# An up projection by Strassen's scheme: seven half-block products in place of eight, in an encoder layer on one core

## The chip, the cores and the metric

The kernel runs on one core of a Trainium2 chip. The metric is the device time of one execution in microseconds (us); three runs of the kernel before took 3004.14, 3004.00 and 2998.63 us, median 3004.0. The engines go by the names of the profile: PE is TensorE (matrix products; PEld is its loading of the stationary operand), DVE is VectorE, ACT is ScalarE, POOL is GpSimd, SP is the engine that issues most DMAs.

## The reference, cut to what matters

The layer is a mixing part (a state-space branch and an attention branch) and a feed-forward part. Only the feed-forward part is changed in what it computes with:

```python
def conv_ffn_sublayer(x, norm_g, w_up, conv_w, conv_b, w_down):
    n = rms_norm(x, norm_g).astype(w_up.dtype)
    h = n @ w_up                                   # (tokens, 1024) @ (1024, 5632)
    h = depthwise_conv3(h, conv_w) + conv_b        # over tokens, zero beyond either end
    g, up = jnp.split(h, 2, axis=-1)               # 2816 + 2816 columns
    act = silu(g) * up
    return x + act @ w_down                        # (2816, 1024)
```

It is applied to a prompt of 256 tokens and to a sample of 2048 tokens with the same weights (2304 tokens in all). Everything is float32.

## The kernel before, in words

A product of two float32 matrices is made of three TensorE products: each operand is split into a high part (rounded to `F32R`) and a low part (what is left), and hi.hi, lo.hi and hi.lo are summed in PSUM (`mm3`, lines 151 to 154). To split costs one ACT copy (high) and one DVE subtraction (low).

After the attention, a stage of the output projection takes the 18 tiles of 128 tokens one by one (`prepare`, `scale_b`, `project_b`, `second_norm`, lines 1213 to 1290; the order is `TOKS`). `second_norm` normalises a tile, transposes it on TensorE (tile `ptn`) and splits it into the tiles `n2a` (prompt and the first 1152 tokens, kept in SBUF) or, for the rest, by way of DRAM into `n2b`.

The up projection (lines 1293 to 1342, tiles named `pu`) then loops over 22 column tiles `ct`, and in each over 5 blocks of tokens: one of 512 columns and four of 450 (with the neighbours that the convolution reads). For each block and each of the two halves `j` (gate and up), 24 matmuls (8 row blocks of the weights, three products each) sum in one PSUM bank; ACT multiplies by the middle tap and adds the bias on the way out of PSUM (L1329), DVE adds the two outer taps straight from PSUM (L1332, L1335), then ACT makes the silu (L1338), DVE the product (L1339), and a DMA writes the result `act_d`. `up_weight` (lines 1170 to 1179) loads one 1024x128 piece of `w_up` (`us`, 512 KB), multiplies it by the norm's gains on DVE (L1176) and splits it (L1177, L1178). It is called for `ct + 1` ahead of the products of `ct`, so each weight is loaded and split once: 44 pieces.

The down projection (tiles named `pf`, lines 1353 to 1386) follows: 2376 matmuls of 512 columns, with `down_weight` for its weights.

All instructions are ordered by a planner at build time that works through a list in the order of the program and gives an engine its next instruction when the operands are ready in its own estimate of time; the order within each engine is fixed from then on, and waits between engines are put in by it. A buffer of a pool (`bufs=`) is reused once all that used it are done.

## Time and profile before

| what | us |
|---|---|
| median of the runs (lowest, highest) | 3004.0 (2998.63, 3004.14) |
| span of the profiled execution | 2999.1 |
| first matmul of the up projection | at 1325.4 |
| first matmul of the down projection, straight behind the last of the up projection | at 2445.1 |
| PE busy in the span | 2901.1 (97%) |
| DVE, ACT, POOL busy in the span | 1555.8, 1048.5, 509.2 |

The profile gives the span of the one execution it was taken in, and no other time for that execution; the span lies inside the spread of the runs. Busy times of PE overlap one another (a matmul is counted from start to the modelled end of its pipeline), so the rate of matmuls is read from how many start in a stretch, not from their durations.

### The profile page before, as it was taken

What the parts mean: (1) busy time and instruction counts of PE and PEld (TensorE: products, weight loads), DVE (VectorE), ACT (ScalarE), POOL (GpSimd) and SP (SyncE); (2) the same over time, 40 slices, a digit from 0 to 9 for tenths busy, and PEclk for the clock granted to TensorE, in tenths of its full rate; (3) what the DMA queues carried; (4) which work ended last, traced back from release to release, by engine and by line L of the source; (5) the groups of instructions that cost most, each with busy time, mean ns of one, the idle gap of its engine ahead of it and who ended that gap; (6) DMA issues with size and microseconds to landing.
All of it is one profiled execution on the core that took longest, in us unless ns stands there. A gap on an engine that the chain in (4) does not pass through costs nothing.

```text
span 2999.1 us, 41529 instructions
## 1 busy us (share of the span) xinstructions
PE 2901.1 (97%) x15224; PEld 2475.5 (83%) x15224; DVE 1555.8 (52%) x4006; ACT 1048.5 (35%) x2390; POOL 509.2 (17%) x946
## 2 busy tenths in 40 slices
PE   7998999989899999999999999999999999999999
PEld 7887777778788887888898989898888888888887
DVE  5766899976644545774444444444444442223221
ACT  3444455445665664452222222222222230002000
POOL 0588433221343343110000000000000000000000
PEclk9998999998999999999999999999999999999999
DMA  7564878595769775664111111111111142224221
GB/s 217 181 222 129 263 223 245 169 222 121 173 155 186 170 167 171 223 202 146 54 37 50 40 51 40 50 39 48 41 44 46 44 154 88 83 84 133 84 80 49
DMA packets 407064, 369.19 MB, mean 123 GB/s; under 512 B 84801, under 2 KB 352717, under 8 KB 403789
## 3 DMA queue, kind: packets, MB, share of 16 engines
q1 hardware_dynamic: 384012, 316.18, 36.2%
q0 software_dynamic: 22848, 50.35, 7.0%
q8 instruction: 121, 1.98, 0.3%
q14 instruction: 83, 0.67, 0.1%
HBM read 228.93 MB, written 137.53 MB: 122 GB/s over the span
## 4 chain that ended last, share of the span: by engine, by line
PE 70%; DMA 4%; DVE 2%; ACT 2%; issue 0%; POOL 0%; SPq 0%; DVEq 0%; ACTq 0%; POOLq 0%
PE pu L153 12%; PE pu L154 12%; PE pu L152 12%; PE pf L153 6%; PE pf L154 6%; PE pf L152 6%; PE po L996 3%; PE pt L149 2%; PE s L959 2%; PE s L960 2%; PE ppa L152 1%; PE ppa L153 1%; PE ppa L154 1%; DMA wsoa<-in_w_out_dram 1%; DMA wb<-w_d 1%; DMA x<-x_d 1%
## 5 line engine op out<-in xcount | busy, mean ns | idle before, releaser
L1332 DVE SCALAR_TENSOR_TENSOR h<-pu,convp,h 128x448 f32<-128x448 f32 (+3 forms) x264 | 162.4, 616 | 554.8 <-ACT h L1329 554.8
L152 PE MATMUL pu<-n2a,uw 128*128 128x450 f32 (+1 forms) x1056 | 398.1, 377 | 0.9 <-ACT n2a L1237 0.9
L153 PE MATMUL pu<-n2a,uw 128*128 128x450 f32 (+1 forms) x1056 | 398.5, 377 | 0.4 <-DVE n2a L1238 0.4
L154 PE MATMUL pu<-n2a,uw 128*128 128x450 f32 (+1 forms) x1056 | 398.1, 377 | 0.0
L1329 ACT ACTIVATE h<-pu,convp 128x448 f32<-128x448 f32 (+2 forms) x220 | 161.9, 736 | 632.5 <-PE pu L154 632.4
L153 PE MATMUL pf<-dw,ah 128*128 128x512 f32 x792 | 310.9, 393 | 0.0
L154 PE MATMUL pf<-dw,ah 128*128 128x512 f32 x792 | 310.5, 392 | 0.0
L152 PE MATMUL pf<-dw,ah 128*128 128x512 f32 x792 | 310.2, 392 | 0.0
L153 PE MATMUL pu<-n2b,uw 128*128 128x450 f32 x704 | 258.8, 368 | 0.0
L154 PE MATMUL pu<-n2b,uw 128*128 128x450 f32 x704 | 258.7, 367 | 0.0
L152 PE MATMUL pu<-n2b,uw 128*128 128x450 f32 x704 | 258.6, 368 | 0.0
L1381 DVE TENSOR_TENSOR acc<-pf,acc 128x512 f32<-128x512 f32 x72 | 49.7, 691 | 390.6 <-PE pf L154 390.6
L153 PEld LDWEIGHTS pu<-n2a,uw 128*128 128x128 f32 x1056 | 199.6, 189 | 28.6 <-DVE n2a L1238 0.8
L152 PEld LDWEIGHTS pu<-n2a,uw 128*128 128x128 f32 x1056 | 198.6, 188 | 28.9 <-ACT n2a L1237 1.1
L154 PEld LDWEIGHTS pu<-n2a,uw 128*128 128x128 f32 x1056 | 199.2, 189 | 27.0
L1367 ACT ACTIVATE ah<-at 128x512 fp32r<-128x512 f32 x72 | 53.0, 784 | 420.5 <-PE pf L154 420.5
L966 ACT ACTIVATE sb<-sb,st 128x256 f32<-128x256 f32 (+2 forms) x384 | 172.3, 451 | 29.7 <-DVE st L965 28.0
L153 PEld LDWEIGHTS pf<-dw,ah 128*128 128x128 f32 x792 | 148.3, 187 | 35.2 <-DVE dw L1192 0.4
L152 PEld LDWEIGHTS pf<-dw,ah 128*128 128x128 f32 x792 | 148.3, 187 | 35.1
L154 PEld LDWEIGHTS pf<-dw,ah 128*128 128x128 f32 x792 | 148.3, 187 | 34.5
L1335 DVE SCALAR_TENSOR_TENSOR h<-pu,convp,h 128x448 f32<-128x448 f32 (+1 forms) x264 | 162.8, 617 | 7.8
L959 PE MATMUL s<-kh,qs 128*128 128x256 f32 (+2 forms) x384 | 151.5, 402 | 0.0
(603 smaller groups left out, 6116.2 us busy)
## 6 DMA issues: line engine op xcount, KB each, us to landing
at<-act_d SPq DMA_DIRECT2D x36, 704.0 KB
us<-in_w_up_dram SPq DMA_DIRECT2D x44, 512.0 KB
qk_d<-qt SPq DMA_DIRECT2D x72, 256.0 KB
act_d<-h SPq DMA_DIRECT2D x66, 224.0 KB
wb<-w_d SPq DMA_DIRECT2D x32, 384.0 KB
ds<-in_w_down_dram SPq DMA_DIRECT2D x44, 256.0 KB
ph_d<-ph SPq DMA_DIRECT2D x16, 640.0 KB
phl<-ph_d SPq DMA_DIRECT2D x16, 640.0 KB
```

The lines of the kernel that those rows point to most:

```text
L149: T.transpose(out, in_, ident[:n, :n])
L152: mm = T.matmul(ps, lhi, rhi, start=first, stop=False)
L153: T.matmul(ps, lhi, rlo, start=False, stop=False)
L154: T.matmul(ps, llo, rhi, start=False, stop=last)
L959: T.matmul(ps[:, c:c + n], qs[:, q], khi[:, keys], start=True, stop=False)
L960: T.matmul(ps[:, c:c + n], qs[:, q], klo[:, keys], start=False, stop=True)
L966: A.activation(sb[:, c:c + n], sb[:, c:c + n], AF.Exp, bias=mn, scale=-1.0, accum_out=den)
L996: T.matmul(po[half * ST:(half + 1) * ST], v, pb_[:s, half * n + j, :], start=j == 0, stop=j == n - 1)
L1329: A.activation(h[:, a:b], ps[:, a:b], AF.Identity, bias=cw[:, 3], scale=cw[:, 1])
L1332: V.scalar_tensor_tensor(h[:, a1 + o:b1], ps[:, a1 + o - 1:b1 - 1], cw[:, 0], h[:, a1 + o:b1], ALU.mult, ALU.add)
L1335: V.scalar_tensor_tensor(h[:, a1:b1 - o], ps[:, a1 + 1:b1 + 1 - o], cw[:, 2], h[:, a1:b1 - o], ALU.mult, ALU.add)
L1367: A.activation(ahl[:, 0, c0:c1], at[:, c0:c1], AF.Copy)
```

## The change

The tokens are taken in three groups of 768 (`GROUPS`: the prompt with tokens 0 to 511, then 512 to 1279, then 1280 to 2047), and the loop over the 22 column tiles runs inside the loop over the groups. In each of the 66 steps the gate and the up tile of a group (2 x 128 columns of weights, 2 x 512 rows, 2 x 384 tokens) are made of seven products of half blocks in place of eight (Strassen's scheme in Winograd's form): each product is 4 row blocks by three matmuls of 384 columns. The sums of weight blocks are made on GpSimd, the sums of token blocks on VectorE and GpSimd once per group, and the results are put together by sums in PSUM, ACT copies and DVE additions into rows `rg` and `ru` of 768 tokens in SBUF. The convolution reads these rows rather than PSUM; the two last columns of a group are kept in `edges` for the next. The gains of the norm go onto the tokens in `second_norm` instead of onto the weights, and that step no longer splits: it multiplies out of PSUM into `raw` (first group) or writes 256 KB pieces to DRAM (other groups). The weights are loaded, summed and split in each of the three groups anew. `TOKS` is in another order. Comments were removed, and a 64-byte pad was added.

```diff
-NSP = 1152
+GT = 768
+GN = GT // 2
+NG = NT // GT
-    TOKS = [16, 17] + list(range(8, 16)) + list(range(8))
+    TOKS = [16, 17] + list(range(4)) + list(range(8, 12)) + list(range(4, 8)) + list(range(12, 16))
+    GROUPS = [[16, 17, 0, 1, 2, 3], list(range(4, 10)), list(range(10, 16))]
-    wp_u = [ctx.enter_context(mkpool(name="wu0", bufs=2))]
+    wp_u = [ctx.enter_context(mkpool(name="wu0", bufs=4))]
+    wst_v = pu.enter_context(mkpool(name="wstv", bufs=2))
+    wsum = pu.enter_context(mkpool(name="wsum", bufs=1))
+    ORDER = (1, 5, 6, 2, 7, 3, 4)
+    def up_weight(nm, ct):
+        w = []
+        for j in range(2):
+            c0 = j * DFF + ct * P
+            s = (wst_u, wst_v)[j].tile([P, KD, P], F32, name=f"us{nm}{j}", tag="us")
+            nc.sync.dma_start(out=s, in_=w_up[0, :, c0:c0 + P].rearrange("(k p) c -> p k c", p=P))
+            w.append(s)
+        a11, a12, a21, a22 = w[0][:, 0:4], w[0][:, 4:8], w[1][:, 0:4], w[1][:, 4:8]
+        sm_ = wsum.tile([P, 4, 4, P], F32, name=f"su{nm}", tag="su")
+        s1, s2, s3, s4 = (sm_[:, i] for i in range(4))
+        G.tensor_tensor(s1, a21, a22, ALU.add)
+        G.tensor_tensor(s2, s1, a11, ALU.subtract)
+        G.tensor_tensor(s3, a11, a21, ALU.subtract)
+        G.tensor_tensor(s4, a12, s2, ALU.subtract)
+        src = {1: a11, 2: a12, 3: s4, 4: a22, 5: s1, 6: s2, 7: s3}
...
+            out[m] = wp_u[i >= 4].tile([P, 2, 4, P], F32R, name=f"uw{nm}{m}", tag="uw")
+            split_in(out[m], src[m])          # ACT copy (high), DVE subtraction (low), 512 columns
...
+    def right_operands(g):                    # token blocks, split_in of 1536 columns each
+        put(1, b11)
+        V.tensor_tensor(b11, b12, b11, ALU.subtract)
+        put(5, b11)
+        V.tensor_tensor(b11, b22, b11, ALU.subtract)
+        put(6, b11)
+        put(2, b21)
+        G.tensor_tensor(b12, b22, b12, ALU.subtract)
+        put(7, b12)
+        put(3, b22)
+        G.tensor_tensor(b21, b21, b11, ALU.subtract)
+        put(4, b21)
...
+            product(p, 1, wt, True, False)
+            A.activation(rg[:, lo], p, AF.Copy)
+            product(q, 5, wt, True, False)
+            A.activation(ru[:, hi], q, AF.Copy)
+            product(p, 6, wt, False, False)
+            A.activation(rg[:, hi], p, AF.Copy)
+            product(t, 2, wt, True, True)
+            V.tensor_tensor(rg[:, lo], t, rg[:, lo], ALU.add)
+            product(p, 7, wt, False, False)
+            V.tensor_tensor(ru[:, hi], p, ru[:, hi], ALU.add)
+            product(q, 3, wt, False, True)
+            V.tensor_tensor(rg[:, hi], q, rg[:, hi], ALU.add)
+            product(p, 4, wt, False, True)
+            A.activation(ru[:, lo], p, AF.Copy)
...
+                A.activation(h[:, a:b], r[:, a:b], AF.Identity, bias=cw[:, 3], scale=cw[:, 1])
+                    V.scalar_tensor_tensor(h[:, c0:c1], r[:, c0 - 1:c1 - 1], cw[:, 0], h[:, c0:c1],
+                    V.scalar_tensor_tensor(h[:, c0:c1], r[:, c0 + 1:c1 + 1], cw[:, 2], h[:, c0:c1],
```

The tile `p` takes four products in turn in one PSUM bank (1, then 6, 7 and 4 added on top); between them it is copied or added out, so the next product on `p` waits for that. `p` and `q` share a pool of 4 banks, `t` has 3. The rows, `h` and the loads of weights have two buffers each, the four weight sums (`wsum`) one, the seven token operands one.

## Rows read from the trace of the kernel before

**Rows 1.** Busy time by stretch: up projection, then down projection.
```profile
core 0: us, PE busy (x) PEld busy (x) DVE busy (x) ACT busy (x) POOL busy (x), PEclk, DMA share, GB/s
1500.00:2400.00 900.00, 900.00 (x4267) 804.75 (x4266) 391.80 (x581) 215.29 (x302) 0.00 (x0) 1.00 0.14 44
2460.00:2990.00 530.00, 529.99 (x2293) 428.90 (x2292) 123.33 (x151) 62.79 (x81) 0.00 (x0) 1.00 0.29 89
```
**Rows 2.** Who waited for whom, longest in total first (engine line <- releaser).
```profile
ACT h L1329 <- PE pu L154: 632.4, 198, 9.8
DVE h L1332 <- ACT h L1329: 554.8, 213, 5.5
```
**Rows 3.** Order of time, attention: TensorE at 256 columns (start, us, engine).
```profile
696.34 0.30 PE L153 MATMUL pg<-zlo,ghi 128*128 128x256 f32 x1
696.36 0.19 PEld L154 LDWEIGHTS pg<-zhi,glo 128*128 128x128 f32 x1
...
696.48 0.28 PE L154 MATMUL pg<-zhi,glo 128*128 128x256 f32 x1
696.49 0.19 PEld L152 LDWEIGHTS pg<-zhi,ghi 128*128 128x128 f32 x1
...
696.60 0.28 PE L152 MATMUL pg<-zhi,ghi 128*128 128x256 f32 x1
696.60 0.19 PEld L153 LDWEIGHTS pg<-zlo,ghi 128*128 128x128 f32 x1
696.72 0.28 PE L153 MATMUL pg<-zlo,ghi 128*128 128x256 f32 x1
```
**Rows 4.** First matmuls of the up and the down projection (ns min/median/max, starts).
```profile
L152 PE MATMUL pu<-n2a,uw x1056: 360/369/482, 1325.4 to 2424.7; 128*128 128x450 f32 x110, 128*128 128x512 f32 x66
L152 PE MATMUL pf<-dw,ah x792: 388/394/400, 2445.1 to 2994.1; 128*128 128x512 f32 x198
```
**Rows 5.** Order of time, end of attention: DVE operations back to back.
```profile
1194.45 0.68 DVE L1035 TENSOR_TENSOR ot<-ot,ot 128x512 f32<-128x512 f32 x1
1195.05 0.74 DVE L165 SCALAR_TENSOR_TENSOR olob<-wsob,gains,ohib 128x512 fp32r<-128x512 f32 x1
1195.72 0.68 DVE L1035 TENSOR_TENSOR ot<-ot,ot 128x512 f32<-128x512 f32 x1
```
**Rows 6.** Groups by line and shape, DVE (count, busy us, mean ns).
```profile
L1381 DVE TENSOR_TENSOR acc<-pf,acc 128x512 f32<-128x512 f32 x72 | 49.7, 691 | 390.6 <-PE pf L154 390.6
L1178 DVE TENSOR_TENSOR uw<-us,uw 128x1024 fp32r<-128x1024 f32 x44 | 53.4, 1215 | 0.0
L1368 DVE TENSOR_TENSOR ah<-at,ah 128x512 fp32r<-128x512 f32 x36 | 24.9, 691 | 0.0
```
**Rows 7.** The same view, ACT.
```profile
L1367 ACT ACTIVATE ah<-at 128x512 fp32r<-128x512 f32 x36 | 22.7, 631 | 420.5 <-PE pf L154 420.5
L949 ACT ACTIVATE pb<-pt 128x384 f32<-128x384 f32 x30 | 14.5, 483 | 8.9 <-DVE pb L950 8.9
L557 ACT ACTIVATE junk<-xt 128x1024 bf16<-128x1024 f32 x18 | 19.0, 1057 | 30.3 <-DMA xt<-in_x_sample_dram 27.4 <-DMA xt<-in_x_prompt_dram 3.0
```
**Rows 8.** POOL: additions of two SBUF operands (line: count, min/median/max ns; groups).
```profile
L1035 POOL TENSOR_TENSOR ot<-ot,ot x30: 1263/1282/1709, 772.7 to 1187.4; 128x512 f32<-128x512 f32 x30
L1257 POOL TENSOR_TENSOR ot<-ot 128x256 f32<-128x256 f32 x18 | 13.3, 737 | 95.8 <-ACT ot L1256 95.8
```
**Rows 9.** Order of time, POOL and DVE beside each other.
```profile
1221.08 0.46 POOL L1258 TENSOR_TENSOR ot<-ot 128x128 f32<-128x128 f32 x1
...
1221.17 0.38 DVE L142 SCALAR_TENSOR_TENSOR rb8t<-rb8y 128x1 f32<-128x1 f32 x1
1221.48 0.15 DVE L142 SCALAR_TENSOR_TENSOR r216t<-r216y 128x1 f32<-128x1 f32 x1
```
**Rows 10.** Lines L165 (both operands in SBUF) and L873 (one in PSUM): min/median/max ns.
```profile
L165 DVE SCALAR_TENSOR_TENSOR olob<-wsob,gains,ohib x8: 739/896/1895, 1175.8 to 1206.3; 128x512 fp32r<-128x512 f32 x8
...
L873 DVE SCALAR_TENSOR_TENSOR pxt<-ppa,rab,pxt x32: 734/749/752, 823.9 to 1198.4; 128x512 f32<-128x512 f32 x32
```
**Rows 11.** Busy time by stretch, columns as in rows 1: the output projection ahead.
```profile
1210.00:1326.00 116.00, 112.60 (x565) 93.78 (x565) 92.56 (x424) 65.22 (x107) 19.18 (x32) 1.00 0.71 232
```
**Rows 12.** Order of time, DVE: a load of weights, waited for.
```profile
2042.29 1.22 DVE L1176 TENSOR_TENSOR us<-us,gains 128x1024 f32<-128x1024 f32 x1 [0.83 <-DMA us<-in_w_up_dram]
```
**Rows 13.** Order of time, SP: the issue of that load.
```profile
2038.47 7.18 SPq L1173 DMA_DIRECT2D us<-in_w_up_dram  x2
```

More of the change, by code (lines that the diff above doesn't have):

```diff
@@ L112, in tile_encoder @@
     x1_d = scratch("x1_d", [NT, D])
[L113 removed]
+    n2_d = [[[scratch(f"n2_d{g}{k}{h}", [P, 4, GN]) for h in range(2)] for k in range(2)] for g in range(1, NG)]
     act_d = scratch("act_d", [NCT, P, NT])
@@ L1189, in down_weight @@
             nc.sync.dma_start(out=s[:, i], in_=w_down[0, r0:r0 + P, h * 512:(h + 1) * 512])
+        if pool is wp_u[0]:
+            for i in range(2):
+                hl = pool.tile([P, 2, 4, P], F32R, name=f"dw{half}{e}{i}", tag=tag)
+                hl = hl.rearrange("p s k c -> p s (k c)")
+                split_in(hl, s[:, i])
+                downw[divmod(e + i, KF)] = hl
+            return
         hl = pool.tile([P, 2, 2, 512], F32R, name=f"dw{half}{e}", tag=tag)
-        A.activation(hl[:, 0], s, AF.Copy)
-        V.tensor_tensor(hl[:, 1], s, hl[:, 0].bitcast(F32), ALU.subtract)
+        split_in(hl, s)
         for i in range(2):
@@ L1288, in tile_encoder @@
         if i == 4:
-            upw = {(0, j): up_weight(0, j) for j in range(2)}
+            upg = up_weight("0_0", 0)
+            upw = next(upg)
     second_norm(*prev)
@@ L1294, in tile_encoder @@
         return
+    wp_u.append(pu.enter_context(mkpool(name="wu1", bufs=6)))
+    n2bp = pu.enter_context(mkpool(name="n2b", bufs=1))
     hpool = pu.enter_context(mkpool(name="hp", bufs=2))
[L1298 to L1302 removed]
@@ new lines, in tile_encoder, with put @@
+    edges = [hpool.tile([P, 2, NCT, 2], F32, name=f"edge{g}", tag=f"edge{g}", bufs=1) for g in range(NG - 1)]
+    right_ops = {}
+    def right_operands(g):
+        (b11, b12), (b21, b22) = raw
+        def put(m, src):
+            pool = n2pool if m in ORDER[:4] else n2bp
+            right_ops[m] = pool.tile([P, 2, 4, GN], F32R, name=f"no{g}{m}", tag=f"no{m}")
+            split_in(right_ops[m], src)
+        put(1, b11)
[9 more added lines that the diff above has]
+        put(4, b21)
@@ new lines, in product @@
+    def product(ps, m, w, first, last):
+        r = right_ops[m]
+        for k in range(4):
+            for i, (a, b) in enumerate(((0, 0), (0, 1), (1, 0))):
+                T.matmul(ps, w[m][:, a, k], r[:, b, k], start=first and k == 0 and i == 0,
+                         stop=k == 3 and i == 2, skip_group_check=True)
+    next(upg)
+    for g in range(NG):
+        right_operands(g)
+        if g + 1 < NG:
+            for k in range(2):
+                for h in range(2):
+                    raw[k][h] = n2pool.tile([P, 4, GN], F32, name=f"rb{g}{k}{h}", tag=f"rb{k}{h}")
+                    nc.sync.dma_start(out=raw[k][h], in_=n2_d[g][k][h])
+        for ct in range(NCT):
+            wt = upw
+            if (g, ct) != (NG - 1, NCT - 1):
+                for upw in up_weight(*((f"{g}_{ct + 1}", ct + 1) if ct + 1 < NCT else (f"{g + 1}_0", 0))):
+                    pass
+            else:
+                for e in (0, 2):
+                    down_weight(0, e, wp_u[0], "uw")
+            rg, ru = [hpool.tile([P, 2 + GT], F32, name=f"r{g}_{ct}{j}", tag=f"r{j}") for j in range(2)]
+            lo, hi = slice(2, 2 + GN), slice(2 + GN, 2 + GT)
+            p = psm.tile([P, 512], F32, name=f"pu{g}_{ct}p", tag="pw")[:, :GN]
+            q = psm.tile([P, 512], F32, name=f"pu{g}_{ct}q", tag="pw")[:, :GN]
+            t = pst.tile([P, 512], F32, name=f"pu{g}_{ct}t", tag="pt")[:, :GN]
+            product(p, 1, wt, True, False)
[12 more added lines that the diff above has]
+            A.activation(ru[:, lo], p, AF.Copy)
+            hv = []
+            a = 1 if g else 2
+            b = GT + 2 if g == NG - 1 else GT + 1
+            for j, r in enumerate((rg, ru)):
+                if g:
+                    G.tensor_copy(r[:, 0:2], edges[g - 1][:, j, ct])
+                if g + 1 < NG:
+                    G.tensor_copy(edges[g][:, j, ct], r[:, GT:GT + 2])
+                cw = convp[:, :, j * NCT + ct:j * NCT + ct + 1]
+                h = hpool.tile([P, 2 + GT], F32, name=f"h{g}_{ct}{j}", tag=f"h{j}")
+                A.activation(h[:, a:b], r[:, a:b], AF.Identity, bias=cw[:, 3], scale=cw[:, 1])
+                for c0, c1 in ((3, 2 + NP), (3 + NP, b)) if g == 0 else ((a, b),):
+                    V.scalar_tensor_tensor(h[:, c0:c1], r[:, c0 - 1:c1 - 1], cw[:, 0], h[:, c0:c1],
@@ L1333, in tile_encoder @@
                                            ALU.mult, ALU.add)
-                    o = 1 if last else 0
-                    V.scalar_tensor_tensor(h[:, a1:b1 - o], ps[:, a1 + 1:b1 + 1 - o], cw[:, 2], h[:, a1:b1 - o],
+                for c0, c1 in ((2, 1 + NP), (2 + NP, b)) if g == 0 else ((a, min(b, GT + 1)),):
+                    V.scalar_tensor_tensor(h[:, c0:c1], r[:, c0 + 1:c1 + 1], cw[:, 2], h[:, c0:c1],
                                            ALU.mult, ALU.add)
```

86 lines of the change are left out of this document (22 added, 64 removed).

## The prediction

> **What bounds the kernel now.** I read the view of busy time by stretch first. In the up projection TensorE is never idle, DVE is busy 44% of the time, ACT 24%, POOL not at all, and the clock is granted in full [rows 1]. The list of waits says the same from the other side: the longest waits are ACT for the last matmul of a block and DVE for ACT [rows 2]. So only the number and the rate of matmuls count here, and everything else hides under them. The rate: 4267 matmuls start in 900 us, 210.9 ns each at a mean of 462.4 columns (one block of 512, four of 450); in the down projection 2293 in 530 us, 231.1 ns at 512 columns [rows 1]. At 256 columns three starts take 0.38 us, 127 ns each [rows 3]. The line through 256 and 512 columns rises 0.408 ns a column and gives 210.9 at 462.4, so it holds in between: at 384 columns a matmul takes 127 + 128 x 0.408 = **179 ns**.
>
> **PE: removed and added.** Before: 22 x 5 x 2 x 24 = 5280 matmuls, 5280 x 0.2109 = 1113.6 us; the stage lasts from 1325.4 to 2445.1 [rows 4], 1119.7 us, so 6.1 us of it are the last tiles of the output projection, woven in. After: 66 steps x 7 products x 12 = 5544 matmuls, 84 a step, 15.03 us a step, 992 us in all. That is 121.6 us less, the most that the change can bring. The seven-for-eight would bring 139 at equal width; the narrower matmul gives some of it back.
>
> Whether a narrower matmul still hides the loading of its weights is the first doubt. In the up projection PEld is busy 804.75 of 900 us, 189 ns for each of 4266 loads [rows 1]; if they were strictly serial, a step could not be under 84 x 0.189 = 15.9 us. But at 256 columns loads of 0.19 us start every 0.12 us [rows 3], so they overlap, and I take 179 ns. The Trainium skill (Trainium Kernel Development and Optimization, Best Practices) would have the distance to the roofline judged by the busy share of LDWEIGHTS; by that rule the stage is at 89% already and the change would bring little. That is a rival below; the rows at 256 columns speak against it.
>
> **DVE per step.** Durations overlap when queued, so I use starts: an addition of 512 columns takes 0.60 us, a scaled addition (scalar_tensor_tensor) 0.67 us [rows 5]; a further column costs (1215 - 691)/512 = 1.02 ns, and an operand in PSUM costs the same as one in SBUF, 691 ns at 512 columns [rows 6]. So a step has seven splits of 512 columns, 7 x 0.60 = 4.2; three additions out of PSUM of 384 columns, 3 x 0.47 = 1.4; four taps of 768 columns, 4 x 0.93 = 3.7; one product of 768 columns, 0.86. Sum 10.2 us of 15.03. Gone is the multiplication by the gains (1.22 us a piece, [rows 12]); the rest is what grew. ACT: seven copies of 0.63, four of 384 columns at 0.48, two taps and a silu of 768 columns at about 0.63 + 256 x 0.83 ns = 0.85 [rows 7], the tap with up to 0.15 more: 4.4 + 1.9 + 2.7, 9 us, 60%: covered, unless it is held by something else.
>
> **POOL per step, and the port.** Four sums of 512 columns at 1.28 us [rows 8], 5.1 us. POOL had nothing to do here, and this is what I look at hardest. A DVE operation on a 128x1 operand takes 0.15 us, but 0.38 when a POOL addition has just begun, and then ends with it [rows 9]. A split with both operands in SBUF takes 739 ns at best and 1895 at worst, which is one POOL addition more; the like with one operand in PSUM never exceeds 752 though POOL works beside it too [rows 10]. So DVE operations with two SBUF operands and POOL additions exclude each other. In the new step 8.8 of DVE's 10.2 us are of that kind. If POOL always runs while DVE is idle or on its PSUM additions, the port is taken 8.8 + 5.1 = 13.9 us and a step stays at PE's 15.03; if DVE waits out every POOL addition, it needs 10.2 + 5.1 = 15.3. Both ends lie around PE's own time. I take 15.3, since [rows 9, 10] show DVE waiting to the end: 66 x 15.3 = 1010. In the first group the taps are cut in two at the prompt's end, four starts more (0.67 - 0.52 = 0.15 each), 0.6 us in 22 steps; half of it counted, 6. The Trainium skill (GPSIMD Engine Reference, 4.1 Engine selection) sends elementwise work to VectorE, with GpSimd about 2 times slower on two inputs; here 1.28 against 0.69, so the trace agrees. With the sums on DVE (4 x 0.60) a step would need 12.6 us of DVE and no port, and PE would bound.
>
> **Between groups.** The seven token operands are split anew: seven splits and two sums of 1536 columns at 0.60 + 1.05 = 1.65, 14.8 us of DVE, and two POOL sums of 1.28 + 1024 x 2.1 ns = 3.5 us (2.1 ns a column from 256 and 512 columns, [rows 8]). Each operand has one buffer, so its split waits for the last step's product on it; the DVE queue holds the last step's convolution behind it, and PE waits for it in turn. From both sides: nothing (the last step's slack and the two row buffers take it) to 21.8 us. With the port as full as above there is no slack: 14.8 plus half of POOL's 7, **18 us**, twice, 36. The loads of the next group's tokens stand in SP's queue ahead of the weights of the next step, and wait until the operands are made; a load of 512 KB is 3.8 us from issue to use [rows 12, 13], and there are two buffers, so this hides within the same 18. At the start of the first group four operands can be made during the output projection, where DVE has 23 us free in 116 [rows 11]; three must wait for its memory, but have four products (8.6 us) of cover. Between 0 and 18, I take 5. The hand-over to the down projection: weights for it could be loaded under the last blocks, now the memory is freed in the last step. One output block of its first tile (33 x 0.231 = 7.6 us) is the price at most, 0 at least; 3.
>
> **The rest.** The output projection loses two ACT copies per tile and gains DRAM writes; PE is busy 112.6 of 116 us there [rows 11], so between 3 us won and as much lost (DVE has then four splits of operands more); 0. The order of tiles changes which rows are ready first, and nothing waits for them by more than that. Weights are read three times, 1 MB in 15 us; the DMA engines are 14% busy here [rows 1], about three and a half times that afterwards: hidden.
>
> **Sum.** 1010 + 6 + 36 + 5 + 3 + 6 = 1066 us, against 1119.7: 54 us less. On the profiled execution 2999.1 - 54 = 2945; the median of the runs is 4.9 above that span, so 3004.0 - 54 = **2950 us**.
>
> **Rivals.** (a) PE bounds throughout: POOL's sums fall into DVE's gaps, boundaries cost 5 us each: 992 + 10 + 6 + 4 = 1012, 2896 us. For it: the two loads (13.9 and 10.2 us) are below 15.03; against: the gaps would have to fit to within 8%. (b) Slower: orders fixed at build time collide. `p` is freed for product 4 by a DVE addition that has one product, 12 x 0.179 = 2.15 us, to be done in, and the earlier products on `p` by ACT copies in the same time. If at its head DVE has a split behind a POOL sum (1.28 + 0.60), a tap (0.93) and its own 0.47, that is 3.3 us and PE loses 1.1 us in a step; with two POOL sums in the way 2.4. Above 16.2 us a step ((1119.7 - 50)/66) the gain is gone; at 17 it is 1122 + 50 = 1172, 52 slower, **3056 us**. For it: POOL's four sums come in a burst once `wsum` is free, and DVE then gets one operation between two of them. Against: PE's wait gives DVE the time to catch up, so it can't build up. (c) Weight loads serial: 66 x 15.9 = 1049, with 36 + 14 it is 1099, 2983 us. (d) The boundaries and SP's queue eat all: two times 45 us, 3004 us.
>
> **How the numbers follow.** Forecast (2920 to 2990) 0.44, (a) 0.22, (b) 0.23, (c) 0.06, (d) 0.05. A difference within 0.2%, 6 us, can't be told from none here. Faster is forecast, (a) and (c), 0.72; same is (d), 0.05; slower is (b), 0.23. The range takes in (a), and (b) to some 16.9 us a step: 2888 to 3048; the forecast alone is 2920 to 2990.
>
> **What would show it.** The rate: 384-column matmuls start 179 ns apart inside a product; 189 would be (c). The port: POOL's sums longer than 1.28 us or DVE splits of 1.2 to 1.9 us; PE's waits in a step are for ACT copies or DVE additions of the rows, under 0.5 us a step in sum for the forecast, none for (a), over 1.2 for (b). Boundaries: two holes on PE of 10 to 20 us in all, waiting for `no`. I am wrong if the step is far from 15.3, and in the reason if PE waits for something else than DVE's and POOL's work: weights in DMA, or ACT held at the head of its queue.

## The result

The changed kernel takes 2952.5 us (median of four runs, 2951.4 to 2956.0) against 3002.3 us of the kernel before on the same chip: a ratio of 0.983 (0.982 to 0.985), 50 us less. The profiled execution spans 2954.2 us, against 2999.1. The forecast was 2950.

The first fence has lines of the changed kernel's page and of its groups: engines with busy time and number of instructions, then the splits of weights (L1180: one operand from the loaded weights `us`, or from the sums `su`) and GpSimd's sums (count | busy us, mean ns | idle before).

```profile
PE 2780.2 (94%) x15488; PEld 2462.3 (83%) x15488; DVE 2039.6 (69%) x4384; ACT 1333.2 (45%) x2925; POOL 1086.4 (37%) x1388
...
L1180 DVE TENSOR_TENSOR uw<-us,uw 128x512 fp32r<-128x512 f32 x198 | 219.4, 1110 | 21.2 <-ACT uw L1179 20.1
L1180 DVE TENSOR_TENSOR uw<-su,uw 128x512 fp32r<-128x512 f32 x264 | 196.3, 753 | 18.1 <-ACT uw L1179 17.5
L1197 POOL TENSOR_TENSOR su<-us 128x512 f32<-128x512 f32 x66 | 109.6, 1660 | 278.7 <-DVE uw L1180 132.2
```

The same split takes 1110 ns from `us` and 753 from `su`. GpSimd's sums run when the weights have just come in, beside the first kind, and these sums take 1660 ns instead of the 1282 of [rows 8]. This is the port, in the place where the prediction looked for it.

The second view is busy time by stretch of the changed kernel (us, busy us and count of each engine, granted TensorE clock, DMA share, GB/s): the output projection, a middle stretch of each of the three groups, and the hand-over to the down projection.

```profile
core 0: us, PE busy (x) PEld busy (x) DVE busy (x) ACT busy (x) POOL busy (x), PEclk, DMA share, GB/s
1210.00:1330.00 120.00, 107.54 (x510) 89.00 (x509) 96.18 (x381) 51.63 (x73) 27.97 (x30) 0.93 0.51 165
...
1420.00:1680.00 260.00, 248.09 (x1406) 243.17 (x1406) 242.77 (x319) 135.96 (x234) 133.69 (x100) 1.00 0.30 92
1770.00:2030.00 260.00, 256.87 (x1475) 255.11 (x1474) 237.78 (x263) 140.64 (x242) 154.83 (x141) 1.00 0.32 100
2110.00:2370.00 260.00, 259.33 (x1494) 258.46 (x1493) 240.26 (x265) 142.86 (x246) 143.78 (x107) 1.00 0.31 99
2400.00:2425.00 25.00, 19.41 (x69) 14.00 (x69) 12.85 (x13) 9.35 (x10) 0.00 (x0) 0.86 0.71 227
```

TensorE, never idle in the up projection before [rows 1], has 12 us of gaps in 260 in the first group, 3 in the second and 1 in the third. DVE went from 44% to 91 to 93% busy. In the third group 1494 matmuls start in 260 us, 174 ns each.

Where the time went is read from the first matmuls of three stages (ns min/median/max of one, first and last start): output projection `pw`, up projection `pu`, down projection `pf`.

```profile
L155 PE MATMUL pw<-ohib,mix x144: 387/389/793, 1213.3 to 1346.4; 128*128 128x512 f32 x144
...
L1355 PE MATMUL pu_0p<-no,uw x144: 334/334/522, 1349.6 to 2100.4; 128*128 128x384 f32 x144
...
L155 PE MATMUL pf<-dw,ah x792: 387/389/792, 2399.4 to 2949.3; 128*128 128x512 f32 x198
```

In the kernel before these three begin at 1206.5, 1325.4 and 2445.1 (the last two in [rows 4]; the first from the same view of `pw`, shown under the run a_late). So:

| stretch | before, us | after, us | difference |
|---|---|---|---|
| up to the output projection | 1206.5 | 1213.3 | +6.8 |
| output projection to first `pu` | 118.9 | 136.3 | +17.4 |
| up projection, first `pu` to first `pf` | 1119.7 | 1049.8 | -69.9 |
| down projection to the end | 554.0 | 554.8 | +0.8 |
| span | 2999.1 | 2954.2 | -44.9 |

The total came out almost as forecast. The parts did not: the up projection won 16 us more than the 54 of the sum, and the output projection, put down at nothing, lost 17. The two errors nearly cancel, so the agreement of the total proves neither.

The steps of the up projection: products of neighbouring steps are woven into each other, so a step is counted here as 84 matmuls in the order of their starts, from the first of them to the first of the next 84. In group 0 the first takes 33.9 us, the others 15.46 on the mean; in group 1 it is 31.1 and 20.0, then 14.84; in group 2 29.6 and 19.3, then 14.72. The smallest is 14.56 throughout, 84 x 173.3 ns.

The longest waits of TensorE from 1150 us to the end (who waited <- on whom: us in total, times, longest):

```profile
PE ptn L152 <- ACT n L1258: 9.6, 3, 4.3
PE pu_0t L1355 <- DVE no L1180: 7.6, 2, 5.5
PE pw L155 <- DVE x L1299: 7.5, 3, 4.5
PE pu_0q L1355 <- DVE no L1180: 6.6, 2, 3.5
PE pssD L1288 <- DVE rb11t L145: 5.9, 1, 5.9
...
PE pu_0p L1355 <- ACT no L1179: 2.2, 1, 2.2
```

`no` are the token operands (the boundaries); `pw <- x` and `pssD <- rb11t` belong to the output projection. `ptn <- n` are the transposes of its last three tiles, waiting for their normalisation; all three waits fall between 1361 and 1375 us, inside the first step of the up projection.

### The profile page after: what moved, and what is told of

Its sections match the earlier page's. It is cut to its first block, busy times and chain, and to the rows that moved or that the text cites. A ratio compares the mean times of both kernels' runs of the same rounds, so it can differ in the third digit from the quotient of the medians.

```text
span 2954.2 us, 43719 instructions
## 1 busy us (share of the span) xinstructions
PE 2780.2 (94%) x15488; PEld 2462.3 (83%) x15488; DVE 2039.6 (69%) x4384; ACT 1333.2 (45%) x2925; POOL 1086.4 (37%) x1388
## 4 chain that ended last, share of the span: by engine, by line
PE 47%; DVE 17%; ACT 4%; DMA 4%; issue 3%; POOL 2%; SPq 0%; ACTq 0%; DVEq 0%; POOLq 0%
PE pf L156 6%; PE pf L157 6%; PE pf L155 6%; DVE uw L1180 4%; PE po L1001 3%; DVE h L1407 3%; DVE h L1410 3%; PE pt L152 2%; PE s L964 2%; PE s L965 2%; PE ppa L155 1%; ACT uw L1179 1%; DVE no L1180 1%; PE ppa L157 1%; PE ppa L156 1%
## 5 line engine op out<-in xcount | busy, mean ns | idle before, releaser
L1179 ACT ACTIVATE uw<-su 128x512 fp32r<-128x512 f32 x264 | 161.7, 624 | 263.3 <-POOL su L1200 148.7
L1180 DVE TENSOR_TENSOR uw<-us,uw 128x512 fp32r<-128x512 f32 x198 | 219.4, 1110 | 21.2 <-ACT uw L1179 20.1
L1197 POOL TENSOR_TENSOR su<-us 128x512 f32<-128x512 f32 x66 | 109.6, 1660 | 278.7 <-DVE uw L1180 132.2
L1180 DVE TENSOR_TENSOR uw<-su,uw 128x512 fp32r<-128x512 f32 x264 | 196.3, 753 | 18.1 <-ACT uw L1179 17.5
L1407 DVE SCALAR_TENSOR_TENSOR h<-r,convp,h 128x255 f32<-128x255 f32 (+3 forms) x176 | 188.5, 1091 | 24.7 <-ACT h L1404 24.7
L1410 DVE SCALAR_TENSOR_TENSOR h<-r,convp,h 128x768 f32<-128x768 f32 (+2 forms) x176 | 178.6, 1027 | 0.4
L1404 ACT ACTIVATE h<-r,convp 128x767 f32<-128x767 f32 (+2 forms) x132 | 135.3, 1026 | 68.2 <-DVE r L1391 68.0
L1179 ACT ACTIVATE uw<-us 128x512 fp32r<-128x512 f32 x198 | 123.0, 625 | 56.5 <-PE pu_1p L1355 12.1
L965 PE MATMUL s<-kl,qs 128*128 128x256 f32 (+2 forms) x384 | 136.9, 367 | 0.0
L970 DVE CUSTOM_DVE_ANT_0 sb<-s,bt 128x256 f32<-128x256 f32 (+2 forms) x384 | 120.6, 357 | 17.8 <-PE pt L152 13.0
L499 POOL TENSOR_TENSOR q<-ph,phs 128x64 f32<-128x64 f32 (+6 forms) x352 | 120.6, 375 | 2.5
```

Source lines behind the costliest of these rows:

```text
L499: E.tensor_tensor(m[r][:, :, :, q].rearrange("p g d n -> p (g d) n"), src[:, g, :, q].rearrange("p g d n -> p (g d) n"), sc, ALU.mult)
L965: T.matmul(ps[:, c:c + n], qs[:, q], klo[:, keys], start=False, stop=True)
L1179: A.activation(dst[:, 0], src, AF.Copy)
L1180: V.tensor_tensor(dst[:, 1], src, dst[:, 0].bitcast(F32), ALU.subtract)
L1404: A.activation(h[:, a:b], r[:, a:b], AF.Identity, bias=cw[:, 3], scale=cw[:, 1])
L1407: V.scalar_tensor_tensor(h[:, c0:c1], r[:, c0 - 1:c1 - 1], cw[:, 0], h[:, c0:c1], ALU.mult, ALU.add)
```

## The experiments

### Whose time is the port's: a_vsum, a_allv, a_dummy

**a_vsum** makes the four weight sums on DVE; GpSimd keeps the two token sums of a group and the copies of two columns.

```diff
-        G.tensor_tensor(s1, a21, a22, ALU.add)
-        G.tensor_tensor(s2, s1, a11, ALU.subtract)
-        G.tensor_tensor(s3, a11, a21, ALU.subtract)
-        G.tensor_tensor(s4, a12, s2, ALU.subtract)
+        V.tensor_tensor(s1, a21, a22, ALU.add)
+        V.tensor_tensor(s2, s1, a11, ALU.subtract)
+        V.tensor_tensor(s3, a11, a21, ALU.subtract)
+        V.tensor_tensor(s4, a12, s2, ALU.subtract)
```

> The changed kernel with the four sums of weight blocks of each step on VectorE in place of GpSimd. Theory port (POOL's additions hold up DVE, and DVE's late addition out of p holds up PE): DVE's splits fall from 1.1 and 0.75 to 0.68 us, DVE has 12.6 us of work in a step of 14.56, the waits of PE for that addition go; the steps of the first group fall from 15.5 to 14.6 us, 18 us in all, and the group boundaries lose some: 2925 to 2938 us. Theory load (DVE is simply too full, and four more operations make it later): steps of 15 us and more in all groups, 2955 to 2985 us.

2904.5 us, 0.968 of before (0.966 to 0.970), below both of the expected ranges: 48 us less than the changed kernel, by giving more work to the engine that was 93% busy. Group 0 of a_vsum by stretch, and its splits of weights in the same stretch:

```profile
1420.00:1680.00 260.00, 259.05 (x1495) 258.73 (x1494) 238.91 (x401) 152.63 (x252) 44.30 (x37) 1.00 0.32 97
...
L1180 DVE TENSOR_TENSOR uw<-us,uw 128x512 fp32r<-128x512 f32 x53 | 36.3, 686 | 9.0 <-ACT uw L1179 8.5
L1180 DVE TENSOR_TENSOR uw<-su,uw 128x512 fp32r<-128x512 f32 x69 | 46.9, 685 | 1.7 <-ACT uw L1179 1.7
```

DVE does 401 operations in the stretch instead of 319 and is busy less, 238.9 us instead of 242.8: both kinds of split take 685 ns now. Every step that isn't next to a boundary takes 14.56 us, in all three groups. What DVE loses to GpSimd's sums is more than the sums cost on DVE itself.

**a_dummy** is a_vsum with four additions a step that GpSimd makes into a tile that nobody reads.

```diff
+        dum = wsum.tile([P, 4, P], F32, name=f"dum{nm}", tag="dum")
+        for x, y in ((a21, a22), (a22, a11), (a11, a21), (a12, a22)):
+            G.tensor_tensor(dum, x, y, ALU.add)
```

> The run with the weight sums on VectorE (2904 us), and besides GpSimd again makes four additions of 512 columns in each step, of the same operands, into a tile that nobody reads. It asks why the sums on GpSimd cost 48 us. Theory port (DVE can't read two SBUF operands while GpSimd adds): the waits come back although nothing depends on GpSimd, and since DVE now has 12.6 us of its own, 12.6 + 5.1 = 17.7 us at most against 14.56: steps of 16 to 17.7 us, 2995 to 3110 us. Theory latency (the splits waited for sums that GpSimd makes at half the speed, and the port is no matter): nothing waits for GpSimd, 2904 us.

3087.9 us, 1.028 of before (1.026 to 1.029), 183 us more than a_vsum, though no result hangs on GpSimd's additions (only the weights' buffers wait for them). The same stretch, the useless additions and the splits beside them (group rows as above):

```profile
1420.00:1680.00 260.00, 231.88 (x1248) 224.84 (x1249) 255.95 (x348) 122.60 (x211) 121.43 (x90) 0.96 0.28 84
...
L1203 POOL TENSOR_TENSOR dum<-us,us 128x512 f32<-128x512 f32 x45 | 73.2, 1626 | 22.7 <-DMA us<-in_w_up_dram 20.8
L1180 DVE TENSOR_TENSOR uw<-us,uw 128x512 fp32r<-128x512 f32 x46 | 38.4, 836 | 1.5 <-ACT uw L1179 1.5
```

DVE is busy 98% of the stretch and gets through fewer operations, 348 for 401; 1248 matmuls in 260 us are 17.5 us a step (over whole groups, beside the boundaries, 16.9 to 17.2). The prediction's two loads, 12.6 us of DVE with its own sums and 5.1 of GpSimd, add up to 17.7. So the two engines exclude each other on additions with both operands in SBUF for the most part, as [rows 9, 10] let one suspect. The later release of the weights' buffers is not what did it: in this stretch DVE waits 3.9 us in all, never for a load, and TensorE waits for DVE's and ACT's work on the rows `r` (12.5 and 11.8 us) and for splits of weights (3.5).

**a_allv** is a_vsum with the two token sums of a group on DVE as well (`b12` and `b21` by `V.` instead of `G.`).

> The changed kernel with all its additions on VectorE: the four sums of weight blocks of a step and the two sums of token blocks of a group, so that GpSimd does nothing but the small edge copies in the up projection. Against the run with the weight sums alone on VectorE (2904 us): there PE still lost 13.9 and 9.7 us at the two group boundaries, and single DVE operations took 4.0 and 4.4 us beside GpSimd's token sums of 3.5 us. Theory port: those go, the boundaries cost 4 to 8 us each, the output projection loses one or two waits of 4 to 5 us less: 2885 to 2895 us. Theory load (the boundary is the DVE's own 14.8 us of splits and sums, and two more operations of 1.7 us add to it): boundaries 14 to 18 us, 2904 to 2912 us.

2903.5 us, 0.967 (0.966 to 0.969): no different from a_vsum, just under the range of the second theory. The boundaries do get cheaper, to between what the two theories had. With F for the floor of 14.56, what the steps around each boundary take beyond it is 22.0 and 19.7 us in the changed kernel, 13.9 and 9.7 in a_vsum, 9.0 and 8.0 in a_allv. But the first step of group 0 grew from 30.8 to 35.3 us and the output projection began 5.5 us later, in work that the edit doesn't touch, so the 6.6 us of the boundaries were lost again ahead of them.

### The output projection and the first step: b_toks, a_late, a_late2

**b_toks** is the kernel before with the new order of tiles (`TOKS`) alone.

> The kernel before with the changed kernel's order of tiles and nothing else. In the changed kernel the first matmul of the output projection came 6.8 us later than before (1213.3 against 1206.5), 4 us of them lost after 1150 us. If the order of tiles does that, it comes 3 to 5 us later here too, and the run takes about 3006 us; if the memory taken by the new pools or the earlier load of weights does, it stays at 1206 and 3002 us.

3004.1 us in its one execution, the kernel before 3004.7 on the same chip, and 116.3 us from the first `pw` to the first `pu` (118.9 before): the order costs nothing. The 17 us are not its doing.

What is new in that stretch are the operands of group 0, made while the last tiles are still being projected. The two token sums of GpSimd in the changed kernel and two of DVE's operations beside them, in order of time (start us, us of one; lines of other engines left out), and DVE's splits of token blocks (ns min/median/max, first and last start):

```profile
1282.17 3.50 POOL L1345 TENSOR_TENSOR rb<-rb,rb 128x1536 f32<-128x1536 f32 x1
1282.27 3.43 DVE L146 TENSOR_TENSOR r29t<-r29t,s 128x1 f32<-128x1 f32 x1
...
1291.81 3.42 POOL L1348 TENSOR_TENSOR rb<-rb,rb 128x1536 f32<-128x1536 f32 x1
1291.86 3.39 DVE L145 SCALAR_TENSOR_TENSOR rb4t<-rb4y 128x1 f32<-128x1 f32 x1
```

```profile
L1180 DVE TENSOR_TENSOR no<-rb,no x21: 1744/1750/4854, 1254.6 to 2086.6; 128x1536 fp32r<-128x1536 f32 x21
```

Two small steps of a tile's normalisation, on one column and 0.15 us long by themselves [rows 9], take 3.4 us and end with GpSimd's sum. All of DVE's queue stands behind them; TensorE's waits of 5.9 us for `rb11t` and 4.5 for `x`, both DVE's work on the tiles, end at 1291.9 and 1297.0. A split of 1536 columns takes 1.75 us at the median and up to 4.9.

**a_late** is a_allv, and the first half of each split of group 0 (the ACT copy) waits for the last tile's `second_norm`, so that no operand is made beside the projection of a tile.

```diff
-    def split_in(dst, src):
+    def split_in(dst, src, behind=None):
-        A.activation(dst[:, 0], src, AF.Copy)
+        hi = A.activation(dst[:, 0], src, AF.Copy)
+        if behind is not None:
+            wait_for(hi, behind)
...
-                V.tensor_tensor(nh, pt, gb, ALU.mult)
+                last_norm[0] = V.tensor_tensor(nh, pt, gb, ALU.mult)
...
-            split_in(right_ops[m], src)
+            split_in(right_ops[m], src, last_norm[0] if g == 0 else None)
```

> The run a_allv with one more edit: the seven token operands of the first group are split only once the last tile is normalised, not beside the output projection. Theory: the work on the operands in the output projection is what makes that stage longer (first matmul of it to first matmul of the up projection 118.8 us before, 136.3 in the changed kernel); then it comes back to 118 to 122 us here, and the first step of the up projection grows to 30 to 40 us, since seven operands take DVE 15 us and PE waits for each: the sum of both within 8 us of a_allv. Rival: the stage is longer because the first products of the up projection no longer fill its waits (before, the first block was woven into the last tiles); then it stays at 130 us or more, and the run is 10 to 20 us slower than a_allv.

2886.7 us, 0.961 (0.959 to 0.963): 17 us less than a_allv. The same stretch in a_allv and then in a_late, and the output projection's matmuls in the kernel before and then in a_late:

```profile
1210.00:1330.00 120.00, 110.14 (x537) 91.81 (x537) 97.08 (x393) 53.32 (x75) 22.96 (x30) 0.96 0.56 185
```

```profile
1210.00:1330.00 120.00, 115.78 (x591) 97.19 (x589) 103.63 (x462) 58.69 (x87) 19.11 (x32) 0.99 0.71 219
```

```profile
L152 PE MATMUL pw<-ohib,mix x144: 387/389/501, 1206.5 to 1324.6; 128*128 128x512 f32 x144
```

```profile
L155 PE MATMUL pw<-ohib,mix x144: 389/389/476, 1208.9 to 1323.8; 128*128 128x512 f32 x144
```

The output projection's own matmuls are over in 115 us again, as in the kernel before (118); in the changed kernel they took 133 (1213.3 to 1346.4), in a_allv 128.5. The operands are now all made after it; the first `pu` starts at 1345.3, 136.4 us after the first `pw`, no sooner than in the changed kernel (136.3). In between TensorE waits 11.2 us for the last tile's normalisation and 4.7 for the ACT copies of the first operands:

```profile
PE ptn L152 <- ACT n L1262: 11.2, 1, 11.2
```

The gain stands in the first step, which has its operands ready: 20.0 us for the 35.3 of a_allv. Together, from the first `pw` to the second step, it is 170 us in the changed kernel (136.3 + 33.9), 166.5 in a_allv and 156.4 in a_late. Of the 18.3 us between the spans of a_allv and a_late the up projection holds 15.5; 4.0 lie ahead of the output projection and 4.0 in the down projection, where no edit was made, and 5.2 were lost between the first `pw` and the first `pu`. To make operands early, on engines that the tiles need, cost about 10 us more than to make them late. This went against my expectation that the wait would only be moved and the total stay within 8 us; that the first `pu` would come no sooner is what the rival had foreseen, together with a slower run, which did not come.

**a_late2** holds the splits only to the last addition of `project_b`, one stage sooner.

> The run a_late with the operands of the first group held back only until the last tile's product is added (its normalisation, transposes and stores come after). There PE lost 11.2 us for the last tile's transposes and 4.1 us for the first operand, with ACT and DVE half idle. Theory: the splits of the first operands fill that, the stage before stays at 116 to 119 us and the up projection begins 5 to 10 us sooner: 2876 to 2882 us against 2887. Rival: the splits hold up the last normalisation instead, and the waits only change place: 2885 to 2892 us.

2890.0 us, 0.961 (0.959 to 0.963), the same as a_late, as the rival had it. Between these two points the waits only change place: the first `pu` starts 119.0 us after the first `pw` in place of 136.4, and the first step takes 37.4 us in place of 20.0, with 156.4 together in both.

### The cut taps: a_uncut

**a_uncut** is the changed kernel without the cut at the prompt's end in group 0 (where the prompt and the sample meet, each is convolved with a column of the other).

```diff
-                for c0, c1 in ((3, 2 + NP), (3 + NP, b)) if g == 0 else ((a, b),):
+                for c0, c1 in ((3, b),) if g == 0 else ((a, b),):
-                for c0, c1 in ((2, 1 + NP), (2 + NP, b)) if g == 0 else ((a, min(b, GT + 1)),):
+                for c0, c1 in ((2, b),) if g == 0 else ((a, min(b, GT + 1)),):
```

> The changed kernel with the two outer taps of the first group in one operation each over all 768 columns: the cut between the prompt and the sample is left out, so the columns next to it are not the reference's. Theory: the four more operations are what makes the steps of the first group 15.5 us where those of the others are 14.7 (they start 0.15 us each, and DVE is 92 percent busy): the steps fall to 14.6 to 14.9 us, 13 to 18 us in all, about 2937 us. Rival (the order of the instructions in that group, or its place behind the output projection): they stay at 15.3 to 15.6, 2952 us.

2934.1 us in its one execution, 18 us less than the changed kernel and near the first theory, and group 0's steps after the first are 14.56 to 15.19 us. So the four starts a step, priced at 6 us in all, cost about 18: without them TensorE's waits for the addition L1389 fall from 11.9 us to 0.6 in the stretch from 1420 to 1680 us (3.1 and 0.7 in the stretches of groups 1 and 2 of the changed kernel). A step of group 0 in the changed kernel shows how (start us, us of one, engine and line; DVE, then GpSimd):

```profile
1516.62 1.39 DVE L1180 TENSOR_TENSOR uw<-us,uw 128x512 fp32r<-128x512 f32 x1
1517.94 3.21 DVE L1407 SCALAR_TENSOR_TENSOR h<-r,convp,h 128x255 f32<-128x255 f32 x2
1521.07 1.77 DVE L1180 TENSOR_TENSOR uw<-us,uw 128x512 fp32r<-128x512 f32 x1
1522.76 1.14 DVE L1410 SCALAR_TENSOR_TENSOR h<-r,convp,h 128x255 f32<-128x255 f32 x2
1523.82 0.54 DVE L1389 TENSOR_TENSOR r<-pu_9p,r 128x384 f32<-128x384 f32 x1
```

```profile
1517.42 1.74 POOL L1199 TENSOR_TENSOR su<-us,us 128x512 f32<-128x512 f32 x1
1519.12 1.48 POOL L1198 TENSOR_TENSOR su<-su,us 128x512 f32<-128x512 f32 x1
1520.67 1.61 POOL L1200 TENSOR_TENSOR su<-us,su 128x512 f32<-128x512 f32 x1
```

The two taps of L1407 end at 1521.15 after 3.21 us; L1410, the same width twice, takes 1.14 once GpSimd is done. The addition L1389, which frees `p` for the next product, stands behind them. TensorE waits for it 0.2 to 1.3 us in nearly every step of group 0, and for nothing else in that stretch:

```profile
PE pu_8p L1355 <- DVE r L1389: 1.3, 1, 1.3
```

### The pad and the matmul rate: a_nopad, b_pad, b_448, m_rate

**a_nopad** takes the pad of 64 bytes a partition (`cst.tile([P, 16], F32, name="pad")`) out of the changed kernel; **b_pad** puts it into the kernel before.

> The changed kernel without its 64-byte pad tile; nothing else differs, so all later tiles lie 64 bytes lower in SBUF. Theory A (the place of the operands in SBUF sets the rate of matmuls): 384-column matmuls start about 179 ns apart instead of 173, the 512-column ones of the down projection 231 to 233 instead of 227; 5544 x 6 + 2376 x 5 ns = 33 + 12 us, of which some 10 us vanish in steps that wait for DVE anyway: 2985 to 2997 us. Theory B (the rate depends on the number of columns and on nothing else): no change, 2952 us.

> The kernel before with the same 64-byte pad tile. Theory A: the 512-column matmuls of the down projection start 227 ns apart (231 before), those of the up projection too (233 before): 2376 x 4.5 + 1056 x 6 ns = 17 us; the 450-column blocks, whose rows begin at all offsets, between nothing and 4224 x 4.5 ns = 19 us: 2966 to 2986 us. Theory B: no change, 3002 us. What it gains is the share of the pad in the 50 us of the change.

Without it the changed kernel takes 2965.8 us, 0.988 of before (0.985 to 0.990); with it the kernel before takes 2991.7, 0.996 (0.995 to 0.998). Both times lie between the two theories. The pad is worth 13 us in either kernel, so of the 50 us some 37 are the scheme's. The section on the change names the pad, and the prediction gave it no price. It does not work where the scheme works: within a product of 384 columns matmuls start between 174 and 175 ns apart in the mean with it and without it (median 173), while in the down projection the rate changes. The down projection's matmuls in a_nopad, to be held beside those of the changed kernel above (median 389 ns), and in b_pad:

```profile
L154 PE MATMUL pf<-dw,ah x792: 388/394/795, 2394.1 to 2959.1; 128*128 128x512 f32 x198
```

```profile
L153 PE MATMUL pf<-dw,ah x792: 387/389/496, 2441.5 to 2981.9; 128*128 128x512 f32 x198
```

**b_448** is b_pad with blocks of 448 columns in place of 450, which leaves out the two neighbouring columns that the convolution takes over a block's edge.

> The kernel before with the 64-byte pad, and blocks of 448 columns in place of 450: the neighbours of a block are left out, so the two columns at each block's ends are not the reference's. What is asked is the rate of a matmul. If the rate is columns / 2.4 GHz plus 13 ns wherever rows begin at multiples of 64 bytes (173 ns at 384 and 227 ns at 512 columns do), 448 columns take 200 ns, against 205.5 at 450 (201 by that rule): 4224 x 5.5 = 23 us less than the padded kernel's 2992, about 2968 us. If the extra 5 ns come with narrow blocks of that width for another reason (a bank, the place of the weights), they take 204 to 205 ns and the run 2986 to 2988 us.

2975.5 us, 0.991 (0.989 to 0.992), 16 us less than b_pad and between the two expected times. 448-column matmuls start 202.7 ns apart, 450-column ones 205.8; the 512-column block went from 229.9 to 227.0. So (4224 x 3.1 + 1056 x 2.9) ns = 16 us. A gain in rate alone comes through in full where TensorE is the bound.

**m_rate** leaves the computation out: chains of 24 matmuls, with the stationary operand shifted by w bytes and the moving one by m bytes from a fixed place.

```diff
+    # chain(name, n, om, ow): 24 matmuls of n columns over 8 blocks of each operand
+    wts[:, ow + k*128 : ow + (k+1)*128]
+    mov[:, om + k*512 : om + k*512 + n]
```

> No encoder: only chains of 24 matmuls of the same kind (F32R, 128x128 stationary, moving operand of 256, 384, 448, 450 or 512 columns), with the first byte of the stationary operand shifted by 0, 32 or 64 bytes (w) and that of the moving one by 0, 32, 64 or 96 bytes (m); the output is not the reference's. In the down projection of the kernel before the moving operands in one half of SBUF went at 233 ns and those in the other at 227, and the 64-byte pad made all 227. Theory moving: at 512 columns the shift of the moving operand by 64 bytes changes 227 to 233 or back, that of the stationary one nothing. Theory stationary: the other way round. Theory neither (the pad works by what lies beside the operands, or by what other engines do then): 227 in all. At 384 columns the kernels ran at 173 with and without the pad: no shift should change it by more than 1 ns. 448 columns 200, 450 columns 201 to 206.

Mean start to start, ns, at 512 columns:

| stationary \ moving | m 0 | m 32 | m 64 | m 96 |
|---|---|---|---|---|
| w 0 | 228.7 | 233.4 | 229.3 | 233.9 |
| w 32 | 233.1 | 226.9 | 233.4 | 229.3 |
| w 64 | 233.3 | 233.0 | 227.7 | 233.4 |

Two of the chains in the trace (name: 512 columns, w, m; first and last start of 24): 5.2 us between the first and the last when both are shifted by 32, 5.3 when the moving one is shifted by 64 instead.

```profile
L98 PE MATMUL c512w32m32b<-mov,wts x24: 388/389/394, 254.1 to 259.3; 128*128 128x512 f32 x24
...
L98 PE MATMUL c512w32m64b<-mov,wts x24: 393/396/399, 259.6 to 264.9; 128*128 128x512 f32 x24
```

None of the three theories holds as it was put. Equal shifts give 227 to 229, most others 233 to 234. Neither operand's place alone decides; the two places relative to each other do, with two pairs (w 0 m 64, w 32 m 96) near the fast end though they aren't equal. Other widths spread likewise: 384 columns 173.3 to 176.7, 448 columns 199.9 to 206.4, 256 columns 113.9 to 119.7. But which pairs are fast differs with the width: at 448 columns equal shifts take 202.3 to 206.4, and w 0 m 64 and w 32 m 96 are the fastest, with 199.9 and 200.3.

## Why the prediction came out right in sum and not in its parts

**The rate of TensorE: mis-sized.** 179 ns at 384 columns was a line through two points; it is 173.3, and the floor of a step 14.56 us, not 15.03: 5544 x 5.7 ns = 31 us. The reason lies in the points. 512 columns were read from the down projection at 231.1, which mixes matmuls of 227 and 233 to 234 ns by the operands' places, as m_rate shows them; 256 columns from three starts of another stage at 127, where m_rate finds 113.9 to 119.7. Both were too high. For the first the operands' places are the reason; for the second they don't suffice, and the rest of it is open. The rule that narrower matmuls give some of the seven-for-eight back was right; the amount was not.

**Weight loads serial (c): out.** PEld is busy 258.46 of 260 us in the third group and the matmuls start 174 ns apart, under the 189 of a load. The Trainium skill (Trainium Kernel Development and Optimization, Best Practices) judges the distance to the roofline by MFU, the share of the peak arithmetic rate, and by the busy share of LDWEIGHTS. By the second of these the stage went from 89% to 99% here while TensorE took 2.19 columns a ns before (462.4/210.9) and 2.21 after (384/174), so the share followed the width of the matmuls. The 70 us came from fewer columns to multiply, which this share can't show.

**The port: right, the size of a step in part by luck.** DVE waits out GpSimd's sums on both SBUF operands; a_vsum takes the sums away and the steps fall to the floor, a_dummy puts useless ones back and a step takes 17 us and more. The size of 15.3 us a step was right for group 0 (15.46, with the cut taps 15.6 foreseen) and too high for the others (14.84 and 14.72). DVE isn't as full as the 15.3 had it: in the third group it is busy 240.26 of 260 us, 13.5 us a step, where 10.2 + 5.1 were counted, so by this estimate it waits out some 3 of GpSimd's 5.1. The splits from `us` are lengthened alike in the three groups (1123, 1145 and 1169 ns in the stretches above); what sets group 0 apart are the cut taps. So rival (a) nearly holds in two groups of three. In group 0 the loss is the one that rival (b) described: TensorE waits for L1389 because DVE stands behind a GpSimd sum, 0.7 us a step on the mean, above the 0.5 that the forecast gave as its sign and below the 1.2 of (b). The 17 us a step and the 3056 us of (b) were far off.

**The cut taps: mis-sized.** 6 us were foreseen, 18 measured in the one execution of a_uncut. Half of 0.6 us a step was counted; the cost was not the starts added but what they made wait: TensorE's waits for L1389, 11.9 us in 260.

**Between groups: the wait right, a term missing.** 22.0 and 19.7 us for 18 foreseen. By the starts of matmuls 15.7 and 12.4 of these are waits, for `no` as named and for the next step's weights `uw`, which DVE splits in the same queue. The other 6.2 and 7.4 have no term in the prediction: behind its holes TensorE is granted the lower clock for a while, and the matmuls start 320 ns apart in place of 173. So it is at the first boundary, after a wait of 5.5 us for the operand `no` of `pu_0t` (columns as in the stretches above; 0.50 is the level of 1.2 GHz):

```profile
1714.00:1719.40 5.40, 5.32 (x17) 5.32 (x18) 5.40 (x6) 1.37 (x3) 4.02 (x3) 0.50 0.07 20
```

The share of GpSimd in a boundary is the larger part: 13.9 and 9.7 without the weight sums, 9.0 and 8.0 without any. The weights' loads stayed hidden, and (d) is out.

**The first step and the output projection: wrong.** The step that failed is "four operands can be made during the output projection, where DVE has 23 us free in 116", with nothing put down for that stage. The free time was there in the sum and not in the place: TensorE was busy 97% of that stretch [rows 11], and each tile's chain goes through DVE, so that a split of 1.75 us, or a step of one column held for 3.4 by a GpSimd sum, makes TensorE wait when it stands in front of a tile's own work. The port, priced for the steps, was not priced here. It is a part of it only: a_allv, without a sum on GpSimd, still takes 131.2 us from the first `pw` to the first `pu`, for 136.3. Up to the first `pu` it cost 17 us where nothing was foreseen, and in the first step 19 (33.9 less the floor) where 5 were. b_toks shows that the order of tiles is innocent, a_late beside a_allv that about 10 of the 36 us come from making operands beside the tiles rather than behind them.

The other part is there in either form, and it is the last tiles more than the operands. Of the 19 us of the first step TensorE waits 9.6 for `n` of the last three tiles and spends some 5.6 on their transposes, which stand between the first products. In a_late it waits 11.2 us for `n` and 4.7 for operands. In the kernel before, where the first block of products runs between these transposes, the wait for `n` is 0.5 us in the whole stage. No run found cover for it in the changed kernel.

**Before the output projection: open in part.** `pw` begins 6.8 us later in the changed kernel. Up to 1160 us TensorE's order of matmuls is the same in both, and the changed kernel is 2.7 us late there; b_toks and the seven runs made from the changed kernel are -1.3 to +3.7 us off at that place, so 2.7 is within what executions differ by. From there on TensorE has its work in another order in the changed kernel, and it loses 4.1 us more. a_nopad and a_uncut have that same order and lose 3.4 and 5.2; the five runs with the weight sums on DVE have a third order and lose 1.1 (a_vsum), 1.7 (a_late), 2.0 (a_late2), 2.7 (a_allv) and 9.9 (a_dummy); b_toks keeps the old order there and gains 1.1. So the loss goes with the order in which the planner put the end of the attention, and not with what the edits touch. Why a_dummy loses so much more than the four others no run tells.

**The hand-over to the down projection: mis-sized, and hidden by the pad.** From the first `pf` to the end it took 0.8 us longer (3 foreseen). Its matmuls are 4.5 ns faster by the pad, 10.7 us over 2376, and that was lost to waits for its weights (4.7 and 2.2 us) and to a granted clock of 0.86 on the mean in the 25 us of the stretch shown above, right behind TensorE's holes, where the kernel before has the clock in full. Beside b_pad, which has the pad and the old hand-over and takes 545.3 us from the first `pf` (2441.5) to the end (2986.8), the hand-over costs 9.5.

**The sum, term by term.** In the up projection the steps beside what is extra took 1049.8 - 19.4 - 22.0 - 19.7 = 989 us where 1016 were foreseen (-27: a lower floor, and a port that holds up TensorE in group 0 above all); the boundaries 42 for 36 (+6); the first step 19 for 5 (+14); for hand-over and last tiles 9 were foreseen and nothing is left here (-9), since the last tiles stand in the first step and the hand-over behind the first `pf`. That is the -16. Ahead of it and behind it stand +17, +7 and +1 that were foreseen at nothing, and -54 became -45. A sum that meets the measured one is no evidence for its terms.

**What beats both kernels** is a_late, with all sums on DVE and the first operands held back: 2886.7 us, 66 us less than the changed kernel and 115 less than the one before.

## What to carry to other kernels

Before work is given to an idle GpSimd, see whether DVE beside it has both operands in SBUF: here DVE is busy 17.2 us a step in a_dummy and 13.4 in a_vsum, so 5.1 us of GpSimd's additions cost it some 4, and DVE could have done them in half of GpSimd's time. Free time of an engine summed over a stretch is no room for early work if each tile's chain passes that engine; hold such work back and compare. And take a matmul's rate from a chain of the same shape, at a known place of its operands, rather than from a line through other stages.

## What the runs showed of the hardware that was not expected

- The start-to-start time of matmuls depends on where the two operands lie in SBUF relative to each other: 226.9 to 233.9 ns at 512 columns, 199.9 to 206.4 at 448, 173.3 to 176.7 at 384. A pad of 64 bytes was worth 13 us of 3000. Which rule of bytes it follows is not settled by these chains.
- GpSimd's copies of 128x2 take 0.18 us at the least, 0.65 at the median and 1.7 at the most in the changed kernel (ns below). That the longer ones are held up by DVE, as DVE's operations are by GpSimd's sums, is not shown.

```profile
L1401 POOL COPY edge<-r x88: 179/645/1717, 1390.1 to 2071.7; 128x2 f32<-128x2 f32 x88
```

- DVE and GpSimd lengthen each other: GpSimd's sum of 512 columns went from 1282 to 1660 ns, DVE's split from 686 to 1110, two taps of 255 columns from 1.14 to 3.21 us, and an operation on one column from 0.15 to 3.43 us.
